# The gates' projection by Strassen's scheme, its partial sums added in DRAM

## The chip, the cores and the metric

The kernel runs on one core of one Trainium2 chip. The metric is the device time of one execution in microseconds (us). Three runs of the kernel before took 1529.23, 1527.44 and 1529.01 us, a median of 1529.01 us. One more execution was profiled. All engine times below come from that one.

The core has these engines: PE (matrix products, with PEld for the load of a stationary 128x128 operand), DVE (vector), ACT (scalar functions and copies out of PSUM), POOL (general vector work) and SP, which here only issues transfers. ACT and POOL can issue transfers too. SBUF is the on-chip working memory with 128 partitions. PSUM is the memory into which PE writes; it has eight banks of 128x512 f32. DRAM is the chip's main memory.

## The reference, cut to what matters

One layer of an encoder, 1024 tokens of width 1024, all in float32. `h` is the normalised input. The part that is changed is the line of `gates`.

```python
h = rmsnorm(x, g_mix[l])
z = h @ w_in[l]                                  # pool channels | q | k | v
y_pool = pool_mixer(u_pool, w_pool_grp[l], pool_scale[l])
y_attn = diff_attention(q, k, v, ...)            # 8 heads, two softmax maps each
gates = sigmoid(h @ w_gate[l] + b_gate[l])       # 1024 x 1024 by 1024 x 2048
merged = (gates[..., :D_MODEL] * (y_pool @ w_branch_pool[l])
          + gates[..., D_MODEL:] * (y_attn @ w_branch_attn[l]))
x = x + merged @ w_out[l]
h2 = rmsnorm(x, g_ffn[l])
x = x + jnp.square(relu(h2 @ w_up[l])) @ w_down[l]
```

## The kernel before, in words

**Digits.** A float32 operand `a` is held as two tiles of the matmul's type: `hi`, a rounded copy made by ACT, and `lo = a - hi`, made by DVE or POOL (`split`, lines 130 to 136). A product is then three matmuls, hi·hi, hi·lo and lo·hi (`mm3`, L153, L154, L155). Nearly every matmul of the program comes from these three lines.

**Stages.** In order of time: (1) attention: the normalised input is transposed into the tiles `hT` (`hT[kp, th, digit]`: features in pairs of 128 rows, `th` the half of the tokens), and eight heads of eight token blocks each run through a pipeline of projection (`z`), normalisation of q and k (`ms`, `qn`; a power and a multiplication on POOL, L477 and L486), transposition (`tk`), scores (`sc`), softmax, transposition (`ta`) and the product with V (`po`). (2) The branch stage: the pool branch (`bp`, 192 matmuls), then the attention branch (`baX`, `baY`), both multiplied by the gates. (3) Output projection (`op`). (4) The MLP (`X`, `Y`, `Z`, `W`, then `Da`, `Db`). The attention branch and the MLP already use a seven-product scheme.

**The gates as fill.** The gates' projection depends on `hT` and weights alone. It is written behind the attention in the program and has a lower priority; the scheduler that lays out each engine's order places its matmuls where PE would have no attention work ready. So it is spread over the eight heads, and what is left runs as one block at the end of attention. The pooling groups (`u`, `yp`) are fill of the same kind. Each engine executes its own list strictly in order.

`gate_cols(c)` makes 128 columns of the gates, `c` from 0 to 15: two loads of 256 KB on SP (`fill_w`), two digit pairs (hi on ACT, lo on POOL, tile `fwgate`), then for each token half 24 matmuls into one PSUM bank (`fill_proj`), an ACT copy with the bias into a tile `go` (L785) and a 256 KB store to `g_dram` issued by ACT (L786). The branch stage loads the values back (`gate_half`, L883), applies the sigmoid on ACT and multiplies on DVE.

**Room.** The fill has one PSUM bank of its own (`ps_f`), and late in the stage borrows the two banks of `z`. `go` and the running sums of the pooling groups share two buffers (tag `fo`), raw weight blocks have two (`fr`). `prepare_weights` runs four units of weight preparation for the attention branch on POOL (`weight_unit`, L816 to L834) at the fill steps in `PREP_AT`. After attention, the row tiles `ry` of the attention's result are loaded into freed weight buffers (`y_scaled`, L218 to L227).

## Time and profile before

| what | value |
|---|---|
| median of three runs | 1529.01 us (1527.44 to 1529.23) |
| the profiled execution's own time | 1530.36 us |
| its span from the first to the last instruction | 1528.6 us |
| mean granted clock of PE | 0.999 |
| gates: matmuls, span | 768, first at 28.4 us, last at 696.7 us |
| first `bp` matmul (branch stage) | 696.9 us |

The page of a profile gives the busy time of each engine, the span in 40 slices, the chain of work that ended last, and groups of equal instructions: line, engine, operation, `written<-read` tiles, shape, count, then busy time and the mean of one, then the idle time of the engine just before them with what ended it. Matmuls overlap in PE, so the mean of one is longer than the distance from one start to the next. "To landing" of a transfer is from its issue to the end of its last write.

### The profile page before, as it was taken

The page shows a single profiled execution, that of the slowest core. Times are in us where ns is not written, and L with a number is a line of the kernel's source. Part 1 is how long each engine was busy: PE and PEld are TensorE (multiplying, and loading weights), DVE is VectorE, ACT ScalarE, POOL GpSimd, SP SyncE. Part 2 cuts the span into 40 slices and gives each one's busy share as a digit, 9 for nine tenths or more (in the row PEclk, how much of TensorE's full clock was granted, in tenths as well). Part 3 has the DMA queues.
Part 4 walks back from the last instruction along what each step waited for, and adds up shares of the span by engine and source line. Part 5 has one row for each costly group of instructions (what it writes and reads, how often), then busy time and mean ns, then how long its engine had stood idle before and what let it go on. Part 6 is the DMA issues. An engine that isn't in the chain of part 4 may idle for free.

```text
span 1528.6 us, 21995 instructions
## 1 busy us (share of the span) xinstructions
PE 1515.5 (99%) x7457; PEld 1306.0 (85%) x7457; DVE 979.3 (64%) x2071; ACT 757.6 (50%) x1567; POOL 325.6 (21%) x413
## 2 busy tenths in 40 slices
PE   8999999999999999999999999999999999999999
PEld 6999999999999999888888887888888888888887
DVE  6666566667666666646578569666665668556572
ACT  6545455545454454454464456555555634333331
POOL 5677433334344342212100120000000000000000
PEclk9999999999999999999999999999999999999999
DMA  7455323223232342727366634454433799537650
GB/s 233 125 167 166 105 63 87 68 82 89 68 92 77 90 131 70 248 89 240 133 213 208 226 117 148 153 181 152 142 134 111 268 326 403 172 124 262 227 193 28
DMA packets 195163, 237.36 MB, mean 155 GB/s; under 512 B 13974, under 2 KB 124523, under 8 KB 195052
## 3 DMA queue, kind: packets, MB, share of 16 engines
q1 hardware_dynamic: 177642, 208.66, 42.2%
q10 hardware_dynamic: 17410, 27.31, 4.7%
q8 instruction: 59, 0.97, 0.3%
q14 instruction: 52, 0.43, 0.1%
HBM read 157.24 MB, written 61.90 MB: 143 GB/s over the span
## 4 chain that ended last, share of the span: by engine, by line
PE 93%; DVE 2%; DMA 2%; ACT 1%; SPq 1%; issue 0%; ACTq 0%; DVEq 0%
PE z L153 6%; PE z L155 6%; PE z L154 6%; PE g L154 4%; PE g L155 4%; PE g L153 4%; PE Da L153 4%; PE Da L154 4%; PE Da L155 4%; PE Db L154 3%; PE Db L155 3%; PE Db L153 3%; PE X L153 2%; PE X L155 2%; PE X L154 2%; PE sc L535 2%
## 5 line engine op out<-in xcount | busy, mean ns | idle before, releaser
L153 PE MATMUL z<-wqkv,hT 128*128 128x384 f32 x512 | 176.6, 345 | 2.5 <-ACT hT L132 2.4
L154 PE MATMUL z<-wqkv,hT 128*128 128x384 f32 x512 | 175.6, 344 | 0.0
L155 PE MATMUL z<-wqkv,hT 128*128 128x384 f32 x512 | 174.8, 342 | 0.1
L546 ACT ACTIVATE s<-s,nm 128x256 f32<-128x256 f32 (+7 forms) x128 | 99.5, 778 | 62.2 <-DVE nm L538 61.4
L153 PEld LDWEIGHTS z<-wqkv,hT 128*128 128x128 f32 x512 | 97.6, 191 | 6.0 <-ACT hT L132 3.3
L153 PE MATMUL g<-hT,fwgate 128*128 128x512 f32 x256 | 100.6, 393 | 0.4 <-ACT hT L132 0.4
L155 PE MATMUL g<-hT,fwgate 128*128 128x512 f32 x256 | 101.0, 394 | 0.0
L154 PE MATMUL g<-hT,fwgate 128*128 128x512 f32 x256 | 100.9, 394 | 0.0
L155 PEld LDWEIGHTS z<-wqkv,hT 128*128 128x128 f32 x512 | 97.4, 190 | 2.8 <-DVE hT L133 0.6
L154 PEld LDWEIGHTS z<-wqkv,hT 128*128 128x128 f32 x512 | 97.6, 191 | 2.2
L477 POOL TENSOR_TENSOR ms<-ms,mhalf 128x4 f32<-128x4 f32 x64 | 69.2, 1081 | 138.3 <-DVE ms L476 137.8
L538 DVE CUSTOM_DVE_ANT_0 s<-sc,dist 128x512 f32<-128x512 f32 (+3 forms) x128 | 73.9, 584 | 38.4 <-PE sc L536 38.2
L133 DVE TENSOR_TENSOR AT<-ta,AT 128x256 fp32r<-128x256 f32 (+1 forms) x160 | 61.2, 392 | 47.8 <-ACT AT L132 47.4
L132 ACT CAST AT<-ta 128x256 fp32r<-128x256 f32 (+1 forms) x160 | 54.1, 349 | 50.0 <-PE ta L578 32.4
L133 DVE TENSOR_TENSOR AS<-s,AS 128x512 fp32r<-128x512 f32 x64 | 45.0, 704 | 37.7 <-ACT AS L132 37.6
L535 PE MATMUL sc<-K,Q 128*128 128x512 f32 (+2 forms) x192 | 68.1, 357 | 0.3 <-DMA Q<-Q 0.3
L536 PE MATMUL sc<-K,Q 128*128 128x512 f32 (+2 forms) x192 | 65.7, 347 | 0.0
L133 POOL TENSOR_TENSOR wqkv<-rqkv,wqkv 128x384 fp32r<-128x384 f32 x60 | 62.0, 1051 | 8.5 <-ACT wqkv L132 7.6
L133 POOL TENSOR_TENSOR fwgate<-frgate,fwgate 128x512 fp32r<-128x512 f32 x32 | 42.7, 1336 | 68.8 <-ACT fwgate L132 58.7
L153 PEld LDWEIGHTS g<-hT,fwgate 128*128 128x128 f32 x256 | 48.1, 188 | 8.9 <-ACT hT L132 0.7
L155 PEld LDWEIGHTS g<-hT,fwgate 128*128 128x128 f32 x256 | 48.1, 188 | 8.7
L154 PEld LDWEIGHTS g<-hT,fwgate 128*128 128x128 f32 x256 | 48.1, 188 | 8.5
(472 smaller groups left out, 4379.8 us busy)
## 6 DMA issues: line engine op xcount, KB each, us to landing
wd<-in_w_down_dram SPq DMA_DIRECT2D x56, 512.0 KB, 5.7
wu<-in_w_up_dram SPq DMA_DIRECT2D x32, 512.0 KB, 4.6
udS<-us SPq DMA_DIRECT2D x64, 256.0 KB, 2.1
ur<-udS SPq DMA_DIRECT2D x32, 512.0 KB, 3.4
rqkv<-in_w_in_dram SPq DMA_DIRECT2D x64, 192.0 KB, 2.7
ud<-u ACTq DMA_DIRECT2D x48, 256.0 KB, 3.0
ur<-ud SPq DMA_DIRECT2D x24, 512.0 KB, 7.3
frgate<-in_w_gate_dram SPq DMA_DIRECT2D x32, 256.0 KB, 2.7
```

The lines of the kernel that those rows point to most:

```text
L132: a = nc.scalar.copy(hi, src)
L133: b = (lo_eng or nc.vector).tensor_tensor(lo, src, f(hi), op=ALU.subtract)
L153: nc.tensor.matmul(ps, lhs_hi, rhs_hi, start=first, stop=False, **kw)
L154: nc.tensor.matmul(ps, lhs_hi, rhs_lo, start=False, stop=False, **kw)
L155: return nc.tensor.matmul(ps, lhs_lo, rhs_hi, start=False, stop=last, **kw).ins
L477: nc.gpsimd.tensor_tensor(ms, ms, mhalf[:, 0:4], op=ALU.pow)
L535: nc.tensor.matmul(dst, Q[:, 1, i, :], rhs, start=True, stop=False)
L536: nc.tensor.matmul(dst, Q[:, 0, i, :], rhs, start=False, stop=True)
L538: nc.vector.tensor_tensor_reduce(out=s[i][:, c : c + w], in0=sc[:, 0:w], in1=dist[:, o0 + c : o0 + c + w], scale=2.0 ** -(h + 1), scalar=B ...
L546: nc.scalar.activation(s[i][:, 0:n], s[i][:, 0:n], AF.Exp, bias=last, scale=-1.0, accum_out=Z[:, i, t : t + 1])
```

## The change

The projection's 1024x2048 weight is cut into eight pairs `p` of column tiles. With `hT` as a 2x2 matrix of quarters (feature halves by token halves; `QUARTERS`), the pair's result is a 2x2 matrix too (column tile by token half), and Strassen's scheme (Winograd's form) gives it by seven products of 4x128 features instead of eight.

- The sums of `hT`'s quarters, T3, T2, T1 and T4, are made once, late in attention, by `form`: two POOL operations, one DVE addition and a digit pair for each of four 128x512 slabs.
- The sums of the weight blocks are made per pair by `weight_sums`: four POOL operations of 128x512; three of the results are stored to `s_dram` and read back later.
- Each product is 12 matmuls (`gate_product`), one ACT copy into a tile `go`, and one transfer to `g_dram`. Product 1 belongs to all four quarters of the result and is stored four times over by one ACT-issued transfer. The other six are added to one, two or three quarters in DRAM by POOL-issued accumulating transfers.
- Order: products 1, 2, 3 of each pair in turn during the heads; then 7, 6, 5 and 4, each for all eight pairs. The lo digits of 1, 2, 3 and 7 are made on POOL, those of 5, 6 and 4 on DVE (`ON_DVE`).
- `go` has three buffers of its own, `fr` four; the U tiles go from 11 to 10, the Q tiles from 3 to 2. The first 50 fill banks come from `ps_f` alone. The weight buffers of attention (`wq`) are closed at the end of the gates and the branch stage's (`wl`) opened in the same room, since T2 and T4 live there; so `ry` and the first `wbp` tiles are now filled only when the products that read T2 and T4 have run.

```diff
-N_U, N_W, N_RAW, N_V = 11, 8, 2, 6
-N_FW, N_FR, N_FO = 4, 2, 2
-N_Q, N_QN = 3, 2
+N_U, N_W, N_RAW, N_V = 10, 8, 2, 6
+N_FW, N_FR, N_GO, N_FO = 4, 4, 3, 2
+N_Q, N_QN = 2, 2
-PREP_AT = (2, 4, 6, 8)
+PREP_AT = (3, 6, 9, 12)
+N_HT = 4
+FORM_AT = {"T2": 6, "T1": 2, "T4": 2}
+IN_W = "T2", "T4"
+ON_DVE = "564"
+N_OWN = 50
-G_FIRST, G_Z = 9, 10
+G_FIRST = 12
...
-    g_dram = dram.tile([2 * D, S], F32, name="g_dram")
+    g_dram = dram.tile([NK, P, 4, 512], F32, name="g_dram")
+    s_dram = dram.tile([NK, 3, P, 4, P], F32, name="s_dram")
...
     def fill_bank(name):
+        nfill[0] += 1
+        if nfill[0] > N_OWN:
+            nfill[1] += 1
+            if nfill[1] % 3:
+                return ps_z.tile([P, 512], F32, tag="z", name=name)
         return ps_f.tile([P, 512], F32, tag="f", name=name)
...
-    def gate_cols(c):
-        ws = fill_w(w_gate, c * P, f"gate{c}")
-        for th in range(2):
-            ps = fill_proj(ws, th, f"g{c}_{th}", spare_bank if c >= G_Z else fill_bank)
-            fo = fo_tile(f"go{c}_{th}")
-            nc.scalar.activation(fo[:, 0:512], ps, AF.Identity, bias=cols[:, c : c + 1])
-            nc.scalar.dma_start(g_dram[c * P : (c + 1) * P, th * 512 : (th + 1) * 512], fo[:, 0:512])
-            yield
+    def form(name, a, b, op):
+
+        for k in range(4):
+            hi, lo = (fr_tile([P, 512], f"t{name}{k}{i}") for i in "hl")
+            (ah, al), (bh, bl) = side(a, k), side(b, k)
+            nc.gpsimd.tensor_tensor(hi, f(ah), f(bh), op=op)
+            nc.gpsimd.tensor_tensor(lo, f(al), f(bl), op=op)
+            nc.vector.tensor_tensor(hi, hi, lo, op=ALU.add)
...
+            split(t[0], t[1], hi)
+            T.setdefault(name, []).append(t)
+
+    PRODUCTS = {
+        "1": ("11", "11", (0, 4, 1)), "2": ("12", "21", (0, 1, 1)), "3": ("S4", "22", (1, 2, 1)),
+        "4": ("22", "T4", (2, 3, 1)), "5": ("S1", "T1", (1, 4, 2)), "6": ("S2", "T2", (1, 4, 1)),
+        "7": ("S3", "T3", (2, 4, 1)),
+    }
...
+    def weight_sums(p):
+
+        a11, a12, a21, a22 = (raw_block(p, n) for n in ("11", "12", "21", "22"))
+        yield a11
+        yield a12
+
+        def made(i, o, x_, y_, op):
+            nc.gpsimd.tensor_tensor(o, x_, y_, op=op)
+            if i is not None:
+                nc.sync.dma_start(s_dram[p, i], o)
+
+        made(0, a22, a21, a22, ALU.add)
+        made(2, a21, a11, a21, ALU.subtract)
+        made(1, a11, a22, a11, ALU.subtract)
+        made(None, a12, a12, a11, ALU.subtract)
+        yield a12
+
+    def gate_product(p, j, src=None):
+
+        a, b, (first, end, step) = PRODUCTS[j]
+        r = src or side_w(p, a)
+        w = digits(r, f"fwg{p}_{a}", nc.vector if j in ON_DVE else nc.gpsimd)
+        ps = fill_bank(f"g{p}_{j}")
+        for k in range(4):
+            hi, lo = side(b, k)
+            mm3(ps, w[:, 0, k, :], w[:, 1, k, :], hi, lo, k == 0, k == 3)
+        go = go_tile(f"go{p}_{j}")
...
+        n = len(range(first, end, step))
+        dst = g_dram[p, :, first:end:step, :]
+        src = go.unsqueeze(1).broadcast_to([P, n, 512])
+        if j == "1":
+            nc.scalar.dma_start(dst, src)
+        else:
+            nc.gpsimd.dma_start(dst, src, accum_op=ALU.add)
...
+    form("T3", "22", "12", ALU.subtract)
+    for _ in range(N_HT):
+        gate_step()
+    for j, then in zip("765", (("T2", "T3", "11", ALU.add), ("T1", "22", "T2", ALU.subtract), ("T4", "21", "T2", ALU.subtract))):
+        for p in range(NK):
+            if p == FORM_AT[then[0]]:
+                form(*then)
+            gate_product(p, j)
+    for p in range(NK):
+        gate_product(p, "4")
     while gate_step():
         pass
-    assert not units_left
-
-    vpool = attn.enter_context(tc.tile_pool(name="vpool", bufs=1))
+    for st_ in (ts[1], ph, hd):
+        st_.close()
+    wpools.append(mix.enter_context(tc.tile_pool(name="wl", bufs=N_W, reuse_waits="tile")))
...
         loaded[f"g{r0}_{th}"] = nc.sync.dma_start(
-            gt, g_dram[r0 * P : (r0 + 1) * P, th * 512 : (th + 1) * 512]
+            gt, g_dram[r0 // 2, :, r0 % 2 * 2 + th, :]
         ).ins
```

The change moves instructions at two places that matter below. The scheduler's lists are quoted without times; a row is source line, operation, written and read tiles, shape.

**POOL, in the middle of the first head.** `ms0_3` and `ms0_4` are the powers for token blocks 3 and 4 of head 0, `qn0_2` and `qn0_3` the multiplications for blocks 2 and 3, `wd` and `wq` the weight preparation. Before:

```order
L477 TENSOR_TENSOR ms0_3_632<-ms0_3_632,mhalf_101 128x4
L816 CAST wd0_0_6575<-wq0_0_6572 128x256 x2
L486 TENSOR_TENSOR qn0_2_579<-qn0_2_579,ggh0_373 128x2x64
L817 TENSOR_TENSOR wd0_0_6575<-wq0_0_6572,wd0_0_6575 128x256 x2
L821 TENSOR_TENSOR wq0_0_6572<-wq0_0_6572 128x256
L833 TENSOR_TENSOR wq0_0_6572<-wq0_0_6572 128x256
L486 TENSOR_TENSOR qn0_3_638<-qn0_3_638,ggh0_373 128x2x64
L816 CAST wd0_0_6575<-wq0_0_6572 128x256
L477 TENSOR_TENSOR ms0_4_696<-ms0_4_696,mhalf_101 128x4
```

The same stretch now (`fr1_..` are the weight sums of pair 1, the `DMA` row adds product 2 of pair 0 to DRAM):

```order
L491 TENSOR_TENSOR ms0_3_636<-ms0_3_636,mhalf_110 128x4
L850 TENSOR_TENSOR fr1_21_6613<-fr1_11_6609,fr1_21_6613 128x512
L500 TENSOR_TENSOR qn0_2_583<-qn0_2_583,ggh0_377 128x2x64
L909 CAST wd0_0_6583<-wq0_0_6580 128x256 x2
L850 TENSOR_TENSOR fr1_11_6609<-fr1_22_6615,fr1_11_6609 128x512
L881 DMA g_dram_137<-go0_2_6551 128x512
L910 TENSOR_TENSOR wd0_0_6583<-wq0_0_6580,wd0_0_6583 128x256 x2
L850 TENSOR_TENSOR fr1_12_6611<-fr1_12_6611,fr1_11_6609 128x512
L500 TENSOR_TENSOR qn0_3_642<-qn0_3_642,ggh0_377 128x2x64
L491 TENSOR_TENSOR ms0_4_700<-ms0_4_700,mhalf_110 128x4
```

Three weight sums and one accumulating transfer now stand between the attention's own operations. From the power of head 0, block 0, to that of head 1, block 0, POOL's list gains 13 weight sums, 4 digits and 4 transfers and loses 10 operations of the weight preparation, which move to later heads.

**POOL, at the end of the gates.** `go7_5` to `go7_4` are the last accumulating transfers, `r7` belongs to the last head's row factors, `wbp` are digits of the pool branch's weights, which PE needs for its first branch products. Now:

```order
L881 DMA g_dram_137<-go7_5_8273 256x1x512
L653 TENSOR_TENSOR r7_6492<-r7_6492,mhalf_110 128x8
L881 DMA g_dram_137<-go0_4_8294 128x512
L654 TENSOR_TENSOR r7_6492<-r7_6492,rz7_6491 128x8
...
L881 DMA g_dram_137<-go6_4_8420 128x512
L881 DMA g_dram_137<-go7_4_8441 128x512
L145 TENSOR_TENSOR wbp0_0_8463<-rbp0_8461,wbp0_0_8463 128x512
L145 TENSOR_TENSOR wbp0_1_8466<-rbp0_8461,wbp0_1_8466 128x512
```

Before, `wbp0` stood well ahead of the last gates' digits on POOL; it now stands behind the transfer of the last product. On PE the last product is followed by eight hi matmuls of `bp0` and `bp1` and 19 of `bp2`, and only then by the matmuls that read the lo digits of `wbp0`.

More of the change, by code (lines that the diff above doesn't have):

```diff
@@ L218, in y_scaled @@
     def y_scaled(d, rbs):
[L220 removed]
+        rw = wpools[-1].tile([P, S], F32, tag="W", name=f"ry{d}")
         nc.sync.dma_start(rw, y_dram[d * P : (d + 1) * P, :])
@@ L789, in gates @@
-    def gates():
-        for c in range(2 * NK - 2):
-            yield from gate_cols(c)
-        for gen in [gate_cols(c) for c in (2 * NK - 2, 2 * NK - 1)] * 2:
-            next(gen)
-            yield
+            yp = go_tile(f"yps{g}_{th}")
+            nc.scalar.activation(yp, ps, AF.Copy, scale=cols[:, 16 + g : 17 + g])
+            nc.scalar.dma_start(p_dram[g * P : (g + 1) * P, th * 512 : (th + 1) * 512], yp)
+    T = {}
+    QUARTERS = {"11": (0, 0), "12": (0, 1), "21": (2, 0), "22": (2, 1)}
@@ L796, in encoder_kernel @@
+    def gates():
+        for p in range(NK):
+            for j, r in zip("123", weight_sums(p)):
+                gate_product(p, j, r)
+                yield
     stored = {}
@@ L1118, in w_room @@
     def w_room(shape, name):
-        return wpool.tile(shape, F32R, tag="W", name=name, bufs=N_W)
+        return wpools[-1].tile(shape, F32R, tag="W", name=name)
     def h_room(shape, name):
```

102 lines of the change are left out of this document (70 added, 32 removed).

## The prediction

> **What bounds the kernel now.** I read the page first: its busy times, its slices and its chain of waits.
>
> ```profile
> PE 1515.5 (99%) x7457; PEld 1306.0 (85%) x7457; DVE 979.3 (64%) x2071; ACT 757.6 (50%) x1567; POOL 325.6 (21%) x413
> ...
> PE   8999999999999999999999999999999999999999
> ...
> POOL 5677433334344342212100120000000000000000
> ...
> PE 93%; DVE 2%; DMA 2%; ACT 1%; SPq 1%; issue 0%; ACTq 0%; DVEq 0%
> ```
>
> PE is busy in every slice and carries 93% of the chain. POOL is at a fifth on average, but at 50 to 70% in the first four slices, the first two heads. Since a busy PE need not be a full one, I asked next for the waits of PE, all that the trace ascribes to another engine or a transfer (waiting group, releaser: total us, count, longest).
>
> ```profile
> PE g_pso L397 <- DMA g_row<-in_g_mix_dram: 3.0, 1, 3.0
> PE z L153 <- ACT hT L132: 2.4, 2, 1.6
> PE hb L1162 <- POOL y L1159: 2.0, 2, 1.0
> PE X L153 <- ACT U L1325: 0.9, 1, 0.9
> PE g L153 <- ACT hT L132: 0.4, 1, 0.4
> ```
>
> The largest sum to under 10 us, most of it outside attention. Then the timeline of PE in the gates' own block shows how dense the work is.
>
> ```profile
> 663.71 0.39 PE L154 MATMUL g<-hT,fwgate 128*128 128x512 f32 x1
> 663.93 0.39 PE L155 MATMUL g<-hT,fwgate 128*128 128x512 f32 x1
> ...
> 665.29 0.39 PE L155 MATMUL g<-hT,fwgate 128*128 128x512 f32 x1
> ```
>
> The second column is the duration, 0.39 us, but the starts are seven steps in 1.58 us, 0.226 us each. So PE's price of a gate matmul is 0.226, not the mean of 0.393 that its group shows. I use 0.226 throughout.
>
> **The change part by part.**
>
> *Removed.* Seven products of eight remain: 8 pairs x 7 x 12 = 672 matmuls instead of 768. PE gives back 96 x 0.226 = **21.7 us**, provided that it stays as full as it is. The granted clock is 1.00 there, so nothing has to be allowed for it.
>
> *POOL in the heads.* The windows from the first power of head 0 to that of head 1, and from there to that of head 2, give (length; then busy time and count of PE, PEld, DVE, ACT, POOL; clock; DMA share; GB/s):
>
> ```profile
> 18.00:92.70 74.70, 72.29 (x404) 65.71 (x405) 49.73 (x141) 41.76 (x116) 51.28 (x71) 0.98 0.56 169
> 92.70:165.30 72.60, 72.60 (x407) 66.35 (x406) 43.92 (x141) 35.29 (x97) 51.72 (x74) 1.00 0.50 157
> ```
>
> The prices on POOL come from the tile `fwgate` (min, median, max in ns) and from the groups of the weight preparation:
>
> ```profile
> L133 POOL TENSOR_TENSOR fwgate<-frgate,fwgate x32: 1265/1292/2201, 25.5 to 673.6; 128x512 fp32r<-128x512 f32 x32
> ...
> L817 POOL TENSOR_TENSOR wd<-wq,wd 128x256 fp32r<-128x256 f32 x28 | 20.6, 738 | 0.2
> L816 POOL CAST wd<-wq 128x256 fp32r<-128x256 f32 x28 | 12.3, 440 | 22.6 <-DMA wa_dram<-wd 15.2 <-DMA wq<-in_w_branch_attn_dram 4.3 <-PE hps L291 3.1
> L821 POOL TENSOR_TENSOR wq<-wq 128x256 f32<-128x256 f32 x12 | 9.3, 778 | 0.2
> ...
> L786 ACTq DMA_DIRECT2D g_dram<-go x32: 325/326/396, 46.5 to 697.8; - x32
> ```
>
> A weight sum has the shape of a digit, so 1.29 us. In head 0 the 13 sums and 4 digits cost 17 x 1.29 = 21.9; three `wq` differences, four casts and three `wd` digits leave, 3 x 0.778 + 4 x 0.440 + 3 x 0.738 = 6.3; net 15.6. In head 1 the same count gives 6.5. Each head also issues 4 accumulating transfers from POOL. No row shows such an issue: ACT's takes 0.33, a whole POOL operation 1.29, and I take 1.0, nearer the latter, since an issue on POOL may have to be worked out by the engine. Together 15.6 + 4 + 6.5 + 4 = 30.1 us. POOL is then at 51.3 + 19.6 = 71 of 74.7 us in head 0, and at 62 of 72.6 in head 1. Idle time is 23.4 and 20.9, so it all fits on paper. But POOL also carries the power and the multiplication of every token block, and a list in strict order that is 95% full passes delays on to `tk`, then to the scores, which PE has only the gates' fill to cover. Bounds: nothing, or half of the 30.1 (15). I take **+4 us**, the part of head 0 that falls within a few per cent of saturation, and nearer to nothing because of the idle time.
>
> *DVE and ACT.* DVE gains 24 digits, 16 additions and 16 splits for the T tiles, ACT 24 copies out of PSUM, 24 hi casts and 16 for `form`:
>
> ```profile
> L937 DVE TENSOR_TENSOR wr<-wr 128x512 f32<-128x512 f32 x2 | 1.4, 683 | 0.0
> L132 ACT CAST fwgate<-frgate 128x512 fp32r<-128x512 f32 x32 | 19.8, 617 | 14.8 <-PE g L155 10.1 <-DMA frgate<-in_w_gate_dram 3.6 <-POOL wd L816 0.8
> L785 ACT ACTIVATE go<-g,cols x32: 667/689/702, 45.8 to 697.1; 128x512 f32<-128x512 f32 x32
> ...
> 610.00:697.00 87.00, 87.00 (x427) 73.23 (x426) 45.65 (x118) 41.23 (x90) 22.42 (x18) 1.00 0.50 165
> ```
>
> That is 56 x 0.69 = 38 us of DVE and 24 x 0.69 + 40 x 0.62 = 41 of ACT, spread over 690 us in which both idle for a third and more: even in the last window DVE is busy for 46 of 87 us. Priced at nothing; PE's own work hides it. The 32 operations of `form` cost POOL 41 us, late in the stage, where it is busy 22 of 87: nothing either.
>
> *The accumulating tail.* Products 7, 6, 5 and 4 run for all pairs at the end of attention, almost back to back on PE. A new `go` can be written only when one of its three buffers has been read out by its transfer, and PE's bank is freed only by that write. Product 6 carries 768 KB to DRAM, product 5 512 KB. In the new order of PE a product 6 comes every 17 matmuls or so, a product 5 every 14: 3.84 + 3.2 = 7.04 us for a pair's 1.31 MB, less the time in which two 256 KB weight blocks are read. What the transfers reach at most in this case, and what loads and plain stores of 256 KB take to landing:
>
> ```profile
> 1250.00:1300.00 50.00, 50.00 (x221) 41.12 (x220) 41.22 (x39) 21.09 (x21) 0.00 (x0) 1.00 1.03 394
> ...
> DMA to landing us min/median/max: 2.0/2.4/3.5
> ...
> frgate<-in_w_gate_dram SPq DMA_DIRECT2D x32, 256.0 KB, 2.7
> g<-g_dram SPq DMA_DIRECT2D x32, 256.0 KB, 3.7
> ```
>
> At 394 GB/s the weight blocks take 1.33 us, which leaves 5.7; the accumulates as plain writes take 3.3: nothing shows. But an accumulate must have the old value too. If it moves at half, 197 GB/s, a pair takes 6.65, and PE waits 8 x (6.65 - 5.7) = **7.5 us**; at a third, 131 GB/s, 8 x (10 - 5.7) = 34. No accumulate stands in the trace; below nothing is excluded, as the transfers are added. I take half, the least that reading besides writing costs.
>
> The Trainium skill ("Collectives: The Full Stack", section "The bandwidth ceiling: the fold count and why AG ≠ RS ≠ AR") says that an add in a transfer needs two source reads, so that the reading side carries double and the rate halves. By it this term is 7.5 us, by the plain stores' rows nothing; no transfer of the trace adds, so no run here shows it yet.
>
> *Buffers and the passage to the branch stage.* One U tile and one Q tile fewer, no other queue in the head being touched. The Q wait in the trace was 0.3 us:
>
> ```profile
> PE sc L535 <- DMA Q<-Q: 0.3, 1, 0.3
> ...
> L133 POOL TENSOR_TENSOR wbp<-rbp,wbp x8: 1288/1514/5717, 612.0 to 730.0; 128x512 fp32r<-128x512 f32 x8
> L153 PE MATMUL bp<-ypT,wbp x64: 389/389/398, 696.9 to 740.0; 128*128 128x512 f32 x64
> L226 DVE SCALAR_TENSOR_TENSOR ry<-ry,gs,rb x8: 1269/1284/2318, 614.8 to 716.5; 128x1024 f32<-128x1024 f32 x8
> ```
>
> At the end of the gates POOL has to wait for the copy of the last product (0.69), issue its transfer and make `wbp0_0`, 3.5 to 4.2 us; PE meanwhile has 8 + 19 matmuls, 6.1 us. Behind the last transfer on POOL stand only these digits. The `ry` tiles wait on SP for T2's and T4's room, but are needed 192 `bp` matmuls, 43 us, later; eight of them cost DVE 8 x 1.28 = 10 us in there, where it is half idle. `r7`, on POOL behind an accumulate, has 34 matmuls (7.7 us) of cover. Bounds: -2 (the gaps that denser fill could close) to +5, one whole slow `wbp` operation. I take **+1**.
>
> *Sum.* 1530.36 - 21.7 + 7.5 + 4 + 1 = 1521.2 us for an execution like the profiled one. That stood 1.35 us above the median of the runs, so 1519.8, rounded to **1520**.
>
> **The rivals.**
>
> *All of it is hidden* (chance 0.14). For it: PE's waits are small now, three buffers absorb a spread of landing times, DMA is half idle in the gates' block (0.50). Against it: a stage of accumulates is nowhere in the trace. 1530.36 - 21.7 - 1.35 = 1507.3; to 1511 counts here.
>
> *POOL sets the pace of the first heads* (0.14). For it: 71 of 74.7 us, and sums placed right between powers and multiplications. Half of 30.1 shows instead of 4: 1530.36 - 21.7 + 7.5 + 15 + 1 - 1.35 = 1530.8, no change. Against it: PE has the gates' fill and the projection of later blocks to put there. It gets likelier if POOL's operations stretch, as single ones in the rows above did, to 2201 and 5717 ns.
>
> The Trainium skill ("SBUF — State Buffer", section "Who interferes with whom") says that a DVE operation with two SBUF inputs and GpSimd's exclude each other; DVE's busier lists here would lengthen POOL's sums. The maxima above agree with it and do not prove it.
>
> *Accumulates starve `go`* (0.28), the slower side. One mechanism: transfers that read, add and write at a third of the peak hold the three `go` buffers; ACT cannot copy, `ps_f` and `z` banks stay full, PE stands. Price 34.4 in place of 7.5: 1530.36 - 21.7 + 34.4 + 4 + 1 - 1.35 = 1547. After the 5 us of the other terms 16.7 of the gain are left; 8 x (1.31 MB / r - 5.7 us) reaches that at r = 168 GB/s, and the change is slower from there down. For it: three buffers are few, and 2.4 us to landing for a plain 256 KB is already long beside 0.69 for the copy. Against it: DMA has half its time free.
>
> *The change does not do what it says* (0.02): the order of PE shows 672 matmuls, so only an unforeseen stall elsewhere counts here; about 1529.
>
> **How the numbers follow.** Forecast 0.42, with 1511 to 1526 as its own range (the tail between nothing and half as much again, the heads 0 to 10). The range of 1507 to 1541 takes in the hidden case, POOL's case and the slower case up to a rate of about 141 GB/s, and leaves some 0.2 out. A change of 0.2%, 3 us, is what can be told from none. Faster: 0.42 + 0.14 and a share of POOL's case, 0.58. Same: the rest of that and the doubtful case, 0.12. Slower: the starving case and the worst of POOL's, 0.30.
>
> **What would show it.** Right: 672 `g` matmuls with 0.226 us between starts; POOL at 70 us in head 0 with head 0 no more than 4 us longer; accumulates of product 6 landing within 4 to 8 us; PE waits for `go` or its bank between products 6 and 5 of some 8 us in all; `bp` beginning some 10 us earlier. Wrong: landing times of 10 us or more with ACT waiting on `go` (starving), head 0 or 1 longer by 8 (POOL), or PE waits on `wbp0` or `ry` after the last gate product.

## The result

The changed kernel takes 1579.47 us (median of four runs, 1576.76 to 1582.85) beside 1528.43 us for the kernel before: a ratio of 1.0335 with an interval of 1.0314 to 1.0357. It is **51 us slower**, where 1520 us was forecast. The profiled execution has a span of 1577.4 us, 48.8 more than before.

### The profile page after: what moved, and what is told of

It reads as the page before. It is cut to its first block, busy times and chain, and to the rows that moved or that the text cites. A ratio compares the mean times of both kernels' runs of the same rounds, so it can differ in the third digit from the quotient of the medians.

```text
span 1577.4 us, 22222 instructions
## 1 busy us (share of the span) xinstructions
PE 1517.7 (96%) x7361; PEld 1295.7 (82%) x7361; DVE 1033.1 (65%) x2127; ACT 789.5 (50%) x1631; POOL 452.5 (29%) x525
## 3 DMA queue, kind: packets, MB, share of 16 engines
q0 software_dynamic: 11008, 20.97, 8.6%
## 4 chain that ended last, share of the span: by engine, by line
PE 79%; DMA 9%; DVE 5%; ACT 2%; issue 2%; POOL 2%; SPq 0%; ACTq 0%; DVEq 0%; POOLq 0%
PE z L165 4%; PE z L167 4%; PE z L166 4%; PE Da L166 4%; PE Da L165 4%; PE Da L167 4%; PE Db L166 3%; PE Db L165 3%; PE Db L167 3%; PE X L165 3%; PE X L166 3%; PE X L167 3%; DMA fr<-in_w_gate_dram 2%; PE op L166 2%; PE op L167 2%
## 5 line engine op out<-in xcount | busy, mean ns | idle before, releaser
L549 PE MATMUL sc<-K,Q 128*128 128x512 f32 (+2 forms) x192 | 71.0, 371 | 16.4 <-DMA Q<-Q 11.9
L881 POOL DMA_DIRECT2D g_dram<-go x48 | 52.3, 1108 | 78.8 <-ACT go L874 44.5
L550 PE MATMUL sc<-K,Q 128*128 128x512 f32 (+2 forms) x192 | 66.2, 349 | 0.0
L549 PEld LDWEIGHTS sc<-K,Q 128*128 128x128 f32 x192 | 36.2, 189 | 26.0 <-DMA Q<-Q 7.6
L500 POOL TENSOR_TENSOR qn<-qn,ggh 128x128 f32<-128x128 f32 x64 | 37.9, 592 | 62.9 <-DVE qn L494 60.1
L165 PE MATMUL op<-wo,mT 128*128 128x512 f32 x128 | 50.2, 392 | 0.0
L167 PE MATMUL op<-wo,mT 128*128 128x512 f32 x128 | 49.8, 390 | 0.0
L166 PE MATMUL op<-wo,mT 128*128 128x512 f32 x128 | 49.8, 390 | 0.0
L614 PE MATMUL po<-AT,V 128*128 128x512 f32 x128 | 49.4, 404 | 0.0
```

Of the source, the lines that this page charges most:

```text
L165: nc.tensor.matmul(ps, lhs_hi, rhs_hi, start=first, stop=False, **kw)
L166: nc.tensor.matmul(ps, lhs_hi, rhs_lo, start=False, stop=False, **kw)
L167: return nc.tensor.matmul(ps, lhs_lo, rhs_hi, start=False, stop=last, **kw).ins
L549: nc.tensor.matmul(dst, Q[:, 1, i, :], rhs, start=True, stop=False)
L550: nc.tensor.matmul(dst, Q[:, 0, i, :], rhs, start=False, stop=True)
L614: nc.tensor.matmul(both, v_hi, a, start=i == 0, stop=False)
```

## The profile after

The page of the changed kernel (busy times, slices of PE, granted clock and DMA, queues, chain):

```profile
PE 1517.7 (96%) x7361; PEld 1295.7 (82%) x7361; DVE 1033.1 (65%) x2127; ACT 789.5 (50%) x1631; POOL 452.5 (29%) x525
...
PE   8899999999999998886999999999999999999999
...
PEclk9999999999999999998999999999999999999999
DMA  7686644434236535999954633644443499637760
...
q0 software_dynamic: 11008, 20.97, 8.6%
q10 hardware_dynamic: 17026, 27.31, 4.7%
...
PE 79%; DMA 9%; DVE 5%; ACT 2%; issue 2%; POOL 2%; SPq 0%; ACTq 0%; DVEq 0%; POOLq 0%
```

PE has 96 matmuls fewer (7361 instead of 7457) and yet a hole in slices 16 to 19, the end of attention; the DMA row stands at 9 from slice 17 to 20. The chain of waits gives 9% to transfers, against 2% before. Windows of three stages show it in numbers (length; busy time and count of PE, PEld, DVE, ACT, POOL; granted clock; DMA share; GB/s), up to the first `bp` matmul; first the kernel before, then the change:

```profile
0.00:150.00 150.00, 143.45 (x770) 128.94 (x771) 96.74 (x280) 81.18 (x218) 100.83 (x165) 0.99 0.55 172
150.00:600.00 450.00, 450.00 (x2533) 412.35 (x2532) 290.30 (x926) 230.67 (x624) 170.42 (x203) 1.00 0.29 85
600.00:697.00 97.00, 97.00 (x482) 82.51 (x481) 51.97 (x141) 45.95 (x102) 27.60 (x23) 1.00 0.49 162
```

```profile
0.00:150.00 150.00, 135.06 (x718) 119.75 (x719) 93.95 (x261) 79.56 (x212) 112.58 (x160) 0.98 0.74 217
150.00:600.00 450.00, 440.39 (x2468) 401.43 (x2468) 311.31 (x955) 244.93 (x651) 250.27 (x281) 0.99 0.45 113
600.00:745.00 145.00, 117.59 (x510) 93.62 (x509) 81.52 (x180) 69.28 (x149) 69.49 (x61) 0.92 0.91 195
```

Before, PE was busy throughout from 150 us on. Now it idles for 10 us of the long middle and for 27 us of the end, where the DMA engines are 91% busy and the granted clock is 0.92. The 91% are a mean. Up to 650 us DVE is busy for 41.76 of 50 us, and only then are the DMA engines full:

```profile
600.00:650.00 50.00, 40.76 (x190) 33.24 (x189) 41.76 (x101) 26.94 (x66) 27.94 (x25) 0.93 0.69 144
650.00:700.00 50.00, 45.68 (x207) 36.43 (x206) 32.68 (x63) 24.96 (x52) 24.36 (x19) 0.97 1.06 219
```

Taking PE's distances from start to start, less the pitch of each shape (0.226 us for 512 columns, and so on), the time lost to pauses and to a lower clock is 27.5 us up to 150 us (18.1 before), 35.7 to 600 us (19.4) and 45.2 to the branch stage (3.0). That is 68 us more, against 21.7 saved: 46, which agrees with the first `bp` matmul at 741.4 instead of 696.9 us:

```profile
L165 PE MATMUL bp<-ypT,wbp x64: 389/389/628, 741.4 to 785.9; 128*128 128x512 f32 x64
```

Of the remaining 4 us, some 2 are the lower clock just behind that first matmul, and some 2 are lost in the first products of the MLP.

The largest waits of PE in the whole execution (waiting group, releaser: total us, count, longest):

```profile
PE sc L549 <- DMA Q<-Q: 11.9, 10, 3.3
PE g L165 <- ACT go L874: 7.7, 2, 7.3
PE g L165 <- ACT fwg_S L144: 5.7, 3, 2.9
PE bp L165 <- ACT wbp L144: 4.6, 1, 4.6
```

The third is digits whose blocks came late. The second and the fourth are copies and digits that stood behind sigmoids on ACT, as the run that moves the sigmoids shows below; those waited for transfers in their turn. The queues between 600 and 745 us, with the median time to landing of some issues there, show how slow these were (row of the queues: packets, MB, share of all DMA engines; of the issues: count, size, us):

```profile
q0 software_dynamic: 7063, 13.65, 56.2%
q1 hardware_dynamic: 11347, 13.89, 32.9%
...
g_dram<-go POOLq DMA_DIRECT2D x8, 768.0 KB, 9.4
...
fr<-in_w_gate_dram SPq DMA_DIRECT2D x8, 256.0 KB, 13.6
```

The adding queue, `q0`, takes 81 of 145 us of all engines for 13.65 MB, 167 GB/s. A plain load of a weight block, 2.7 us before, lands after 13.6. Since these loads share four `fr` buffers, a late landing also delays the next issue: from 684 to 709 us SP issues seven of them, each in 0.4 us, and stands at waits in between. The longest in sum, up to 745 us, is for earlier blocks to land:

```profile
SPq L832 <- DMA fr<-in_w_gate_dram: 10.5, 3, 4.2
```

## The experiments

Four theories were told apart. D: the adding transfers fill the DMA engines. G: the three `go` buffers are too few. P: POOL's weight sums pace the heads. S: ACT stands at sigmoids whose gate values come late. A fifth, V, concerns the forming of T1 to T4, and a sixth, C, the clock of PE behind a pause. All times are medians of four runs, unless said otherwise; the kernel before took 1527.6 to 1528.1 us beside them, and ratios are to it. The cuts of the edits are marked by `...`; lines that only name an instruction for the order are left out.

### Plain transfers

```diff
-            nc.gpsimd.dma_start(dst, src, accum_op=ALU.add)
+            nc.gpsimd.dma_start(dst, src)
```

> The changed kernel, with the 48 transfers of products 2 to 7 written plainly instead of added (the gates are then overwritten, not summed); their number, size, queue and order stay. Theory D (the DMA engines are full at the end of attention because an adding transfer costs them more than twice a plain one): in the trace of the change the adding queue moved 13.65 MB in 56.2% of 145 us, 167 GB/s; at the 368 GB/s of the plain stores (27.31 MB in 4.7% of 1577 us) the same bytes need 37 us instead of 81, so the DMA share of the end falls below 0.7, PE's stall of 42 us there falls to some 8, and the whole comes to 1532 to 1545 us. Theory P (POOL's weight sums and issues set the pace): both stay as they are, so nothing falls by more than 10 us: 1570 or more. Theory G (three buffers for the product copies are too few, whatever the rate): the buffers come free sooner too, so G alone expects what D expects; it is told apart by the run with two buffers.

Measured: 1549.56 us, ratio 1.0148 (1.0125 to 1.0171), **30 us less** than the change. The adding queue's row becomes:

```profile
q0 software_dynamic: 5888, 20.97, 3.6%
```

3.6% of 1547 us is 56 us of all engines for 20.97 MB, 377 GB/s. The same bytes as additions took 8.6% of 1577, 136 us, 155 GB/s: an addition goes at 0.41 of a plain store. PE's waits for `Q<-Q` fell from 11.9 to 3.7 us. D carries more than half of the loss; P had allowed 10 us at most. The time stayed 5 us above the range that D had given. An issue also became cheaper for POOL, 0.69 instead of 1.09 us (medians), which is 20 us of POOL over 48 issues; the run with 41 us more work on POOL, below, shows how little of such time reaches PE.

### Fewer bytes, as many transfers

```diff
-        "4": ("22", "T4", (2, 3, 1)), "5": ("S1", "T1", (1, 4, 2)), "6": ("S2", "T2", (1, 4, 1)),
-        "7": ("S3", "T3", (2, 4, 1)),
+        "4": ("22", "T4", (2, 3, 1)), "5": ("S1", "T1", (3, 4, 1)), "6": ("S2", "T2", (1, 2, 1)),
+        "7": ("S3", "T3", (2, 3, 1)),
```

> The changed kernel, with products 5, 6 and 7 each added to one quarter of the result instead of two, three and two: the number of transfers stays at 48, their bytes fall from 21 to 12.6 MB, at the end of attention from 16.8 to 8.4. Theory D: at about 160 GB/s half of the end's 105 us of adding transfers go, so its stall falls from 42 us to some 10 to 15: 1545 to 1557 us. Theory P or a cost by the number of transfers: 1572 us or more.

Measured: 1559.68 us (1.0196 to 1.0233), 20 us less, 3 us above D's range. With 40% of the adding bytes gone, two thirds of what plain transfers gave came back. So the bytes are what costs, and a cost by the number of transfers alone is ruled out; that the cost is in proportion to the bytes is not shown.

### Two `go` buffers

```diff
-N_FW, N_FR, N_GO, N_FO = 4, 4, 3, 2
+N_FW, N_FR, N_GO, N_FO = 4, 4, 2, 2
...
-        return fr_tile([P, 512], name) if nbank[1] % 7 % 2 == 0 else go_tile(name)
+        return fr_tile([P, 512], name) if nbank[1] % 3 != 1 else go_tile(name)
```

The branch stage's loads, which share these tiles, are spread over six instead of seven.

> The changed kernel with two buffers for the product copies instead of three. Theory G (the buffers bind): in the row of products 7 and 6 a copy is held for its transfer of 8 to 9 us to landing, so two buffers give one product per 4.5 us or so against 3.84 of matmuls; the end of attention gets longer by 15 us or more: 1594 us or more. Theory D (the DMA engines are full, whoever waits at them): two buffers keep the adding queue as full as three, so 1577 to 1588 us.

Measured: 1583.24 us (1.0339 to 1.0394), 4 us above the change, with overlapping intervals. G, which expected 15 us or more, is refuted for this kernel: it is not the number of buffers that limits. More than three buffers were not tried.

### Without the weight sums on POOL

```diff
-            nc.gpsimd.tensor_tensor(o, x_, y_, op=op)
             if i is not None:
                 nc.sync.dma_start(s_dram[p, i], o)
```

> The changed kernel without the 32 weight sums on POOL (the unsummed blocks take their place, transfers and all else as they are). Theory P: the stretch up to 150 us, which lost 9 us more to pauses of PE than before, and the middle of attention, which lost 16 more, get most of that back: 1555 to 1562 us. Theory D: POOL's sums lie in its idle time, and the heads' losses are those of transfers that land late, so 1573 to 1580 us.

Measured: 1599.62 us (1.0457 to 1.0492), **20 us slower** than with the sums; neither theory had that. A wait of SP up to 700 us in this run, and one of PE:

```profile
SPq L851 <- DMA fr<-in_w_gate_dram: 27.5, 19, 4.1
```

```profile
PE sc L549 <- DMA Q<-Q: 23.5, 11, 6.7
```

Without the sums the scheduler lined up the loads of four blocks and the stores of three of them back to back on SP. A store then waits on SP until its block has landed, and the transfers of Q and K stand behind it. PE waits for Q twice as long as in the change, 23.5 us instead of 11.9. That the order on SP is the cause is likely but not shown, since in the change SP waits as long at the same stores, there for POOL's sums (up to 700 us):

```profile
SPq L852 <- POOL fr L850: 28.1, 14, 5.2
```

So the run can't speak for or against P: it changed the order on SP besides the work on POOL. The row raises another way in which the sums could pace the heads, over SP's queue. With plain transfers the same row is 26.8 us, yet PE's waits for Q are 3.7 us in all; so by itself it costs PE little.

### The sums on POOL, alone

```diff
+            if name[:4] == "gate" and int(name[4:]) < 8:
+                for _ in range(2):
+                    nc.gpsimd.tensor_tensor(rw, rw, rw, op=ALU.add)
             w = fw_tile([P, 2, 4, P], f"fw{name}_{j}")
```

This is an edit of the kernel before with 672 gate matmuls, which is the run after the next.

> The kernel before with 672 gate matmuls (1512 us), plus 32 POOL additions of 128x512 in the first heads, two on each raw weight block of the first eight gate columns ahead of its digits (these columns come out scaled): POOL gets 41 us more work at nearly the place where the change has its weight sums, 17 of the additions in the first head, and DMA, DVE and PE get none. Theory P: half of what is left unexplained between 1512 and the 1527.6 us of the run without adding transfers and without T sums, 6 to 10 us, so 1518 to 1522 us. Against it: 1510 to 1515 us.

Measured: 1520.91 us (0.9939 to 0.9969), 9 us above 1511.98, as P's number had it. But the trace puts the loss elsewhere. First the waits of PE up to 60 us, then from 600 us on:

```profile
PE hps L291 <- DVE hn L284: 2.8, 3, 1.7
PE hps L291 <- DVE hT L133: 2.6, 1, 2.6
```

```profile
PE bp L153 <- ACT wbp L132: 6.5, 2, 5.6
```

In the first 50 us PE loses 4.0 us more than without the additions; in the 100 us after that it gains 3.4 back, and the branch stage begins 2.3 us earlier (677.8 instead of 680.1 us). The 6.5 us are a wait inside the pool branch that comes from the order on ACT. There the cast of `wbp` stands behind a sigmoid that waited for 4.65 us itself. So 41 us of POOL work cost PE about 1 us in the heads: P's number came out, its mechanism did not. What the work on POOL costs while DVE and the DMA engines are as busy as in the change, this run doesn't show.

### The sums on DVE

```diff
-            nc.gpsimd.tensor_tensor(o, x_, y_, op=op)
+            nc.vector.tensor_tensor(o, x_, y_, op=op)
```

> Sigmoids moved, transfers written plainly, and the 32 weight sums on DVE instead of POOL: 41 us of POOL become 22 of DVE. Beside 1542.6 us. Theory P (POOL's sums pace the first heads, where up to 600 us PE loses 10 us more than in the kernel before with 672 matmuls): 1534 to 1539 us. Against it: 1540 us or more.

Measured: 1559.38 us (1.0185 to 1.0234). Beside 1542.62 us, the run with plain transfers and moved sigmoids that is described below, that is 17 us worse than on POOL. PE's longest wait is now one of 5.1 us for `hn`, the normalised input that DVE makes; POOL was the better place.

### 672 matmuls and nothing else

```diff
+        nk = NK - 1 if name[0] == "g" else NK
-        for k in range(NK):
+        for k in range(nk):
```

> The kernel before, with the last of eight feature blocks of every gate product left out: 672 gate matmuls instead of 768, and nothing else of the change. All theories: the 21.7 us of PE show in full, since PE has no pauses: 1506 to 1509 us. If PE's share of the saving is hidden by something else in the kernel before, 1515 us or more.

Measured: 1511.98 us (0.9878 to 0.9907), 15.7 us less than before, not 21.7. The branch stage begins 16.8 us earlier. Fewer fill matmuls leave PE with more uncovered waits (20.8 us lost up to 150 us, against 18.1). So this is what the smaller number of matmuls gives in the order of the kernel before.

### Sigmoids behind the last copies

```diff
-            nc.scalar.copy(go, ps)
+            marks["lastgo"] = nc.scalar.copy(go, ps).ins
...
-        nc.scalar.activation(gt, gt, AF.Sigmoid, bias=zero)
+        sg = nc.scalar.activation(gt, gt, AF.Sigmoid, bias=zero).ins
+        queue_behind(sg, marks["lastgo"])
+        queue_behind(sg, marks["bp01h"])
```

What led to it: ACT's timeline in the changed kernel, SP's and PE's beside it.

```profile
713.23 0.62 ACT L144 CAST fwg<-fr 128x512 fp32r<-128x512 f32 x1
722.92 1.28 ACT L999 ACT_TABLE_LOAD   x1 [9.07 <-DMA g<-g_dram]
724.22 0.72 ACT L999 ACTIVATE g<-g,zero 128x512 f32<-128x512 f32 x1
724.85 0.57 ACT L874 COPY go<-g 128x512 f32<-128x512 f32 x1
```

```profile
711.58 0.32 SPq L996 DMA_DIRECT2D g<-g_dram  x1
```

```profile
725.47 0.79 PE L165 MATMUL g<-TT_0h,fwg 128*128 128x512 f32 x1 [7.29 <-ACT go L874]
```

ACT stood for 9 us at the first sigmoid of the branch stage. Its operand is read back from DRAM by a load that SP issued at 711.58 us and that landed some 11 us later. The copy that frees PE's bank stood behind it. Of the five such loads up to 745 us, the trace has only one wait, of 2.4 us, for an addition to land first:

```profile
SPq L996 <- DMA g_dram<-go: 2.4, 1, 2.4
```

So it is the slow load, more than the wait for the last addition that S names, that held ACT.

> The changed kernel with the sigmoids of the branch stage put behind the last product's copy and the first pool weights' hi digits on ACT; nothing else moves on that engine before. Theory S (ACT, which works in strict order, stands at a sigmoid for 9.07 us and at three more for 3.5 to 4.8 because their gate values come back from DRAM only after the last addition to them, and the copies of product 4 and the digits of the pool weights stand behind): PE's pauses of 7.45 and 4.79 us go, and with them the lower clock that follows, some 5 us: 1579.5 minus 10 to 17, 1562 to 1570 us. Theory D alone (the same transfers are still to be made before the end, so the copies then wait for a buffer instead): 1575 to 1581 us.

Measured: 1573.36 us (1.0273 to 1.0315), 6 us less; between the two theories. The waits of ACT and PE in this run between 690 and 750 us say why:

```profile
ACT go L874 <- DMA g_dram<-go: 17.0, 8, 5.1
```

```profile
PE bp L165 <- ACT wbp L144: 6.4, 1, 6.4
```

The copies no longer stand behind sigmoids, but now they wait 17 us for `go` tiles whose additions have not landed. S was real, and the slow additions take its place. In this order the number of `go` buffers could matter again; that was not tried.

### Both, and then without T1 to T4

The edit of the first run and that of the last together:

> Sigmoids moved and the 48 transfers written plainly (the gates are overwritten, not summed). If the two causes are separate, PE's pause of 5.3 us ahead of the pool branch, which the run with plain transfers alone still had, goes with the clock loss after it: 1549.6 minus 5 to 8, 1541 to 1545 us. If that pause was a transfer's, 1548 to 1551.

Measured: 1542.62 us (1.0078 to 1.0128), 7 us less than with plain transfers alone, as two separate causes would have it; the single runs of the two overlap (1540.36 to 1549.57, and 1546.86 to 1555.37). Then the sums were left out, once with the adding transfers and once with plain ones:

```diff
-        "4": ("22", "T4", (2, 3, 1)), "5": ("S1", "T1", (1, 4, 2)), "6": ("S2", "T2", (1, 4, 1)),
-        "7": ("S3", "T3", (2, 4, 1)),
+        "4": ("22", "21", (2, 3, 1)), "5": ("S1", "22", (1, 4, 2)), "6": ("S2", "11", (1, 4, 1)),
+        "7": ("S3", "12", (2, 4, 1)),
...
-    form("T3", "22", "12", ALU.subtract)
...
-            if p == FORM_AT[then[0]]:
-                form(*then)
```

> The run with the sigmoids moved, and besides without forming the sums T1 to T4: the products read plain quarters of the input (the gates come out different), so 32 POOL operations, 16 DVE additions and 32 digit operations go. Theory V (DVE, busy for 42 of 50 us from 600 us on, where T1 and T4 are formed with additions of up to 2.2 us, paces the last head): 8 us or more less than the run with the sigmoids moved alone. Theory D: within 3 us of it, since the transfers stay, and they may even come closer together.

> Sigmoids moved, transfers written plainly, and the sums T1 to T4 not formed (the products read plain quarters of the input; the gates come out different). Beside 1542.6 us with the sums. Theory V, in a second form (forming the sums is a limit of its own that showed nothing while the adding transfers filled the DMA engines): the stretch from 600 to 650 us, where PE loses 12 us to pauses against 3 in the kernel before with 672 matmuls, gets 6 to 9 of it back: 1533 to 1537. If forming the sums is covered: 1540 to 1545.

Measured with adding transfers: 1573.78 us (1.0286 to 1.0336), no change from 1573.36. With plain ones: **1527.64 us** (0.9986 to 1.0010, ten runs), 15 us less than 1542.62, and more than the 6 to 9 that V had given. Two windows, with plain transfers, first with T1 to T4, then without:

```profile
600.00:650.00 50.00, 43.94 (x205) 34.80 (x203) 45.44 (x93) 29.49 (x67) 29.94 (x27) 0.97 0.63 219
650.00:700.00 50.00, 48.28 (x213) 39.06 (x212) 25.90 (x55) 25.83 (x54) 17.33 (x22) 0.97 0.87 293
```

```profile
600.00:650.00 50.00, 48.59 (x231) 39.71 (x230) 36.34 (x86) 27.37 (x59) 9.45 (x13) 1.00 1.03 365
650.00:700.00 50.00, 50.00 (x235) 41.49 (x235) 21.88 (x52) 27.82 (x55) 12.66 (x19) 1.00 0.73 245
```

While T1 to T4 are formed, DVE is 91% busy (45.44 of 50) and PE loses 6 us of 50; without, DVE has 36 and PE is nearly full. So forming the sums is a limit of its own; which of its parts it is, DVE's additions, POOL's or ACT's casts, was not taken apart. As long as additions fill the DMA engines it costs nothing extra: without the sums, but with adding transfers, PE is busy for 41.54 of the first 50 us while the DMA share is 1.07.

### Additions spread over the heads

```diff
             nc.scalar.dma_start(g_dram[c * P : (c + 1) * P, ...], fo[:, 0:512])
+            nc.gpsimd.dma_start(g_dram[c * P : (c + 1) * P, ...], fo[:, 0:512], accum_op=ALU.add)
```

> The kernel before with 672 gate matmuls (1512 us), where each of the 32 copies is stored as before and then added once more to the same place by a transfer that POOL issues (the gates come out doubled): 8.4 MB of adding transfers, 54 us of all DMA engines at 155 GB/s, spread over the heads where the DMA share is 0.3 to 0.6. Theory D says that it is the full engines that cost, so spread out they cost 1510 to 1517 us. Rival: an adding transfer costs wherever it is, by the late landings of Q and K: 32 of 80 units at the 31 us that plain transfers gave back are 12 us, 1522 us or more.

Measured: 1519.90 us (0.9939 to 0.9972), 8 us above 1511.98, between the two. In the trace the branch stage begins at 678.3 us, 1.8 earlier than without the additions, and PE waits for Q 0.6 us in all up to 600 us. So 32 additions in the heads cost attention nothing; what was lost came later. This trace is of the fastest of the four runs (1515.60 us). As to attention that agrees with D; the median lies 3 us above D's range, and the later loss was not followed up.

### Products 4 and 5 stored plainly

```diff
-        "4": ("22", "T4", (2, 3, 1)), "5": ("S1", "T1", (1, 4, 2)), "6": ("S2", "T2", (1, 4, 1)),
+        "4": ("22", "T4", (4, 5, 1)), "5": ("S1", "T1", (5, 6, 1)), "6": ("S2", "T2", (1, 4, 1)),
...
+        elif j in "45":
+            nc.gpsimd.dma_start(dst, src)
...
+        i = r0 % 2 * 2 + th
+        if i:
+            g2 = tmp(f"gp{r0}_{th}")
+            nc.sync.dma_start(g2, g_dram[r0 // 2, :, 4 if i == 2 else 5, :])
+            nc.gpsimd.tensor_tensor(gt, gt, g2, op=ALU.add)
```

> The run with the sigmoids moved (1573.4 us), and products 4 and 5 stored once each, plainly, in places of their own; the branch stage loads them as well (24 more loads of 256 KB) and POOL, which has little to do there, adds them to the sums before the sigmoid. It computes all that the reference asks. Adding transfers fall from 80 to 56 units of 256 KB, those after 600 us by more than a third. Theory D: plain transfers for all 80 gave 31 us, so 24 of 80 give a third of it, at the place where it counts rather more: 1559 to 1565 us. The rival: the additions are only moved, and 31 us of POOL work and 6 MB of loads delay the branch stage by as much: 1571 us or more.

Measured: 1569.54 us (1.0250 to 1.0298), 4 us less than 1573.36; both theories are half right. The first row of `bp`, first with the sigmoids moved alone, then in this run, and a window and a wait of this run:

```profile
L165 PE MATMUL bp<-ypT,wbp x64: 389/389/793, 732.6 to 778.1; 128*128 128x512 f32 x64
```

```profile
L165 PE MATMUL bp<-ypT,wbp x64: 387/389/632, 713.9 to 760.6; 128*128 128x512 f32 x64
```

```profile
740.00:800.00 60.00, 54.16 (x219) 43.32 (x218) 51.80 (x65) 24.88 (x42) 22.64 (x15) 0.91 0.67 238
```

```profile
PE baX L165 <- DVE mp L252: 4.0, 1, 4.0
```

Attention ends 18.7 us earlier, as D says. From the first `bp` to the end the kernel then needs 10 us more (1562.6 - 713.9 = 848.7 against 838.6): PE waits for gates that are loaded twice and added. DVE, which shares the stage with POOL's additions, is slower there too: its `ry` operations take 1965 ns on average in this window, 1273 in a like one with the sigmoids moved alone. The profiled execution won 8.6 us, the median 4.

### A pause filled with useless matmuls

```diff
-            ps = proj_T(ps_fn(f"bp{d}_{th}"), ws, lambda k, th: pair(ypT[k][th]), th, nk=4)
+            ps = ps_fn(f"bp{d}_{th}")
+            if d == 0 and th == 0:
+                for _ in range(26):
+                    y0 = pair(ypT[0][0])[0]
+                    nc.tensor.matmul(ps, y0[:, 0:P], y0, start=True, stop=True)
+            ps = proj_T(ps, ws, lambda k, th: pair(ypT[k][th]), th, nk=4)
```

> The run with the sigmoids moved, and 26 matmuls without use (26 x 0.226 = 5.9 us) in the place of PE's pause of 6.4 us ahead of the first pool branch product. Theory C (a pause of PE of over 2 us is followed by some 3.5 us at about half the granted clock): with the pause filled, the 4 us behind it run at a granted clock of 1.00, against 0.7 to 0.85 in the run without; the time moves by 2 us or less. If the lower clock has another cause, it stays under 0.9 there.

Measured: 1573.22 us (one run), no change, with these windows; first without the useless matmuls, then with them:

```profile
732.00:736.00 4.00, 3.42 (x8) 2.74 (x9) 0.00 (x0) 3.97 (x7) 3.41 (x3) 0.50 1.07 248
736.00:740.00 4.00, 4.00 (x14) 3.18 (x14) 0.00 (x0) 2.30 (x5) 2.50 (x2) 0.73 0.93 282
```

```profile
732.00:736.00 4.00, 4.00 (x19) 3.34 (x18) 0.00 (x0) 2.54 (x4) 2.31 (x3) 1.00 0.88 218
736.00:740.00 4.00, 4.00 (x19) 3.30 (x19) 0.00 (x0) 3.84 (x7) 1.95 (x3) 1.00 1.06 220
```

The granted clock, the third number from the right, is 0.50 and 0.73 behind the pause, and 1.00 where the pause was filled, at an equally busy DMA. C is shown, by one run: PE's own idleness lowers its clock. The time did not move, as C had it.

## Why the prediction was wrong

Taken away one after the other, the causes add up. 672 matmuls alone give 1512 us; 16 us above that are not traced to one cause, 15 are the forming of T1 to T4, 7 ACT's order and 30 the adding transfers: 1580. The shares hold for this order of taking away, since a cause can cover another.

**96 matmuls, 21.7 us.** The price of a matmul was right; its full effect was not. 15.7 us came out of it when nothing else changed, since the matmuls also cover waits in the heads.

**The accumulating tail, +7.5 us: the step that failed.** "If it moves at half, 197 GB/s" was near: the runs show 155 GB/s over the kernel and 167 in the tail, below the 168 that the prediction itself named as the point where the gain is gone. But its sum let the additions have the engines for themselves, beside two weight blocks per pair. In the tail the other queue moved 13.9 MB as well, a third of the engines' time. By the prediction's own formula 167 GB/s give 8 x (7.84 - 5.7) = 17 us; plain transfers gave back 30, some 8 of them before 600 us by PE's distances, where the prediction had no cost of additions at all. So the term was too small by 22 us: about 10 by the rate, the rest by what the additions cost in the heads and beside the loads of the tail, which no run took apart. The Trainium skill ("Collectives: The Full Stack", section "The bandwidth ceiling: the fold count and why AG ≠ RS ≠ AR") has the rate of a ring's reduction halved against a copy; 0.41 was measured here.

**The rival that starves `go`** had the right sign and the right cause, a low rate of the additions, and for the most part the wrong place. ACT did wait for `go` in the tail, but for 8.1 us in all, and two buffers instead of three cost 4 us. What starved besides were the weight blocks, whose loads landed after 13.6 us, the transfers of Q and K, and whatever was to be read back from `g_dram`.

**ACT priced at nothing.** The prediction followed POOL's list past the last product, and let ACT's go. There the sigmoids of the branch stage stand ahead of the last copies and of `wbp`. Now their operands come back through the full DMA engines, after 9.6 us (median of five loads there), and ACT waits. Taking them out of the way gave 6 and 7 us in two settings; "+1" for the passage was too small by about that.

**DVE and `form` priced at nothing.** "PE's own work hides it" held only because PE was waiting for transfers anyway. With plain transfers it is 15 us. The window that had been quoted, DVE at 46 of 87 us, is an average of a kernel without this work; from 600 to 650 us DVE is at 42 of 50 in the change, and at 45 with plain transfers and moved sigmoids. Its additions also stretch. Rows of DVE, then of POOL, in the changed kernel:

```profile
629.45 2.19 DVE L814 TENSOR_TENSOR tT11h<-tT11h,tT11l 128x512 f32<-128x512 f32 x1
```

```profile
629.35 1.73 POOL L813 TENSOR_TENSOR tT12l<-hT,TT_2l 128x512 f32<-128x512 f32 x1
```

Such an addition takes 0.68 us in 9 of its 16 instances, and up to 2.19 where POOL works on two SBUF tiles at the same time. That agrees with the Trainium skill ("SBUF — State Buffer", section "Who interferes with whom"), which the prediction had brought in for the heads only.

**POOL in the heads, +4 us.** The prediction's own sign for this rival, a head longer by 8 us, did come. From the first power of head 0 to that of head 1 it takes 88.2 us instead of 74.7, and POOL is busy for 72 of them:

```profile
17.52:105.69 88.17, 80.65 (x441) 71.69 (x442) 59.14 (x160) 48.13 (x131) 71.94 (x82) 0.98 0.74 216
```

But PE puts more fill there, 441 matmuls instead of 404, and heads 2 and 3 are shorter, 66.0 and 67.2 us instead of 75: head 4 begins at 316.8 us, at 316.0 before. In the run with the sums on POOL alone the same stretch takes 83.8 us, and PE loses about 1 us up to 600 us. So POOL does pace the first head, and the fill covers nearly all of it. The +4 stands for something that cost less, as far as that run goes.

**The clock, "nothing has to be allowed for it".** In the changed kernel's trace the granted clock stands at 0.50 in eight stretches, the last just behind the first `bp`, for 34 us together; that is 17.1 us of clock, against 1.7 before. A part of it lies in the pauses themselves. The rest is contained in the losses above: each of the eight pauses of 2.2 us or more up to there is followed by at least one stretch of 3.4 us at half the clock, 1.7 us on top.

**What stays open.** Plain transfers, moved sigmoids and no T sums leave 1527.6 us, 15.6 above the kernel with 672 matmuls. Of the excess in the traces, 18 us, 11 lie before the branch stage, mostly in the first 200 us, where PE waits 3.2 us for `hn` and up to 3.3 at once for Q, each with its clock loss; the rest lies behind it, where the first MLP products wait for digits. Neither was tested by itself. Both versions that still compute what the reference asks and won something, with moved sigmoids and with products 4 and 5 stored plainly, stay above 1569 us; none that was tried beats the kernel before.

## What to carry to other kernels

A scheme that saves multiplications on a saturated PE moves its additions to engines and queues; price those in the stage where they bunch, together with all other traffic there, and not by an average. Follow every strict queue past the end of the changed stage: an early instruction of the next stage whose operand now lands late blocks all that stands behind it. And a removed bottleneck should be tested with the next one in mind: forming the sums cost nothing until the transfers were cheap.

## What the runs showed of the hardware

- An adding transfer to DRAM ran at 155 GB/s of all DMA engines, a plain one of the same bytes, from the same queue, at 377. The same bytes were 11008 packets as additions and 5888 as plain transfers. 256 KB took 5.2 us to landing instead of 3.2 (medians), and POOL spent 1.09 us on an issue instead of 0.69.
- With the DMA engines 91% busy, over half of it by additions, a plain load of 256 KB landed after 13.6 us (median of 8) instead of 2.7 (median of 32).
- Idleness of PE halves its granted clock, in the change for 3.4 us or a whole multiple of it; in its trace all these stretches begin a multiple of 3.41 us apart. The Trainium skill ("TensorE: Matmul & The Clock Gate", section "What's actually happening") puts the drop after an idle window of about 3.4 us that runs freely, and the rate then at a half. The rate and the length agree. But a drop here followed a pause of only 2.2 us of PE that had a lone pair of matmuls (a transposition) and 0.5 us of idleness ahead of it, in the first of these windows; the length of a pause alone does not decide, since with the useless matmuls two pauses of 2.2 us were followed by none:

```profile
624.00:628.00 4.00, 1.58 (x11) 1.07 (x9) 3.68 (x10) 1.22 (x3) 3.36 (x4) 1.00 0.78 139
628.00:632.00 4.00, 3.68 (x10) 2.95 (x11) 4.00 (x9) 2.04 (x6) 2.84 (x4) 0.64 0.47 54
```
